# A two-layer decoder trunk: the written order of the feed-forward input stage extended to its first block and to the output stage's first loads, and one product moved to another PSUM bank

## The chip, the cores and the metric

The kernel runs on one core of one Trainium2 chip. A core has TensorE (matrix products, written PE in the profile, its weight loads PEld), VectorE (DVE), ScalarE (ACT), GpSimd (POOL), SyncE (SP) and 16 DMA engines that SP, POOL and ACT feed through queues of their own. On-chip data lies in SBUF, products land in PSUM, which has eight banks of 512 float32 per partition. The metric is the time of one execution on the device in microseconds, lower is better.

## The reference

Two decoder layers over 512 positions of width 1024. Each layer has a mixer, a cross attention into 256 memory rows and a SwiGLU feed-forward part, each between two RMS norms. All of it is float32. The change touches the feed-forward part:

```python
def swiglu(h, w_gu, w_down):
    g, u = jnp.split(h @ w_gu, 2, axis=-1)
    return (jax.nn.silu(g) * u) @ w_down

# in each layer:
h = rmsnorm(x, g_ffn_pre[layer])
y = swiglu(h, w_ffn_gu[layer], w_ffn_down[layer])
x = x + rmsnorm(y, g_ffn_post[layer])
```

`w_gu` is 1024 x 5632 (2816 gate and 2816 up columns), `w_down` 2816 x 1024.

## The kernel before

**Products.** To keep float32 accuracy each operand is split into a rounded high part (a cast on ACT, "hi") and the rest (a subtraction on DVE, "lo"), and each product is three matmuls, high by high, high by low, low by high (`mm3`, lines 299 to 301).

**The feed-forward input stage** computes g and u, transposed, in blocks of 256 columns: 11 blocks of the gate and 11 of the up half, numbered jp 0 to 10. Block 0 of both is computed by `ws_gemm_split` while the rows of the cross attention before it are still being normed and transposed. Its two results end in `act(0, ...)`: a Silu on ACT and a multiply on DVE for each of two halves, and a store of the product y to DRAM from POOL's queue.

**The stream.** The other 20 blocks ("chunks", gate and up in turn) go through `Winograd.stream`, which computes a 2 x 2 block product with 7 products in place of 8. One factor is made of sums of the transposed rows h: n1, n3, s2, n4 (`sums`, 4 subtractions, each with a split into hi and lo), once for all chunks. The other is made of sums of the chunk's weights: t3, t2, t1, t4 (`prepare`, line 432, DVE), split into four pairs hi1 to hi4 (ACT, line 441) and lo1 to lo4 (DVE, line 442). `hi1`/`lo1` hold b11 and t1, the first and third product's weights; `hi2`/`lo2` t2; `hi3`/`lo3` t3 and t4; `hi4`/`lo4` b21 and b22. While the products of one chunk run, the next chunk's weights are prepared, and the chunk after that is loaded from DRAM on SP (`wr`, two loads of 512 KB).

The seven products of a chunk, in order, are a11 b11, s2 t2, n1 t1, n3 t3, a12 b21, a22 t4, n4 b22, each 12 matmuls of 256 columns. They write halves of four banks, `bks[0]` to `bks[3]`; gate chunks use four banks named bB, up chunks four named bA. DVE combines them: q and then u and v (line 455), and the four quarters of the result (`out`: line 827 for gate, 835 for up). Quarter (0, two) reads the fifth product, quarter (0, one) the sixth, and quarter (1, both) the seventh and the third, as `tail` at the start of the next chunk. A gate chunk ends in a Silu on ACT (829), an up chunk in a multiply on DVE (837) and a store of y to DRAM (810).

**The output stage** (`OutProj`, final product with `w_down`) runs y as the stationary operand against 512 weight columns. In `half0_steps` it takes the 22 rows of blocks two at a time: `load_w` loads and splits 512 KB of weights, and `parts`, called `LEAD` = 2 steps ahead, loads back 512 KB of y and splits it. Both come over SP's queue into the pool `wst` of four staging buffers, which the stream also uses for t3 and t4 (`tt`) and for y before its store (`yr`).

**What sets the order.** TensorE's instructions stand in the order in which the code issues them. Inside `stream` that holds for ACT and DVE too (`manual_schedule`): the names that `do(...)` lists between the products are their queue order. Elsewhere a scheduler orders ACT, DVE and the queues by its own estimates, and the pools decide which buffer a tile gets and what it must wait for. Each engine takes its queue strictly in turn.

Of the kernel before, what the change touches and what calls it, by code (L numbers as in the profile page):

```python
# [15 lines left out]
P = 128  # L16
# [9 lines left out]
LEAD = 2  # L26
# [16 lines left out]
def trunk_kernel(ctx: ExitStack, tc: tile.TileContext, a: dict, out: bass.AP):  # L43
# [32 lines left out]
    def f(ap):  # L76
        return ap.bitcast(F32)
# [295 lines left out]
    class Winograd:  # L373
# [7 lines left out]
            self.hT = hT  # L381

        def sums(self):
            hT = self.hT
            r0, r1 = hT.raw
            e, l = slice(0, 256), slice(256, 512)
            a21, a11, a22, a12 = r0[:, :, e], r0[:, :, l], r1[:, :, e], r1[:, :, l]
            sub = lambda o, i0, i1: nc.vector.tensor_tensor(out=o, in0=i0, in1=i1, op=ALU.subtract)
            self.parts = {}
            sub(a22, a21, a22)  # L390
            sub(a21, a21, a11)
            sub(a11, a11, a22)
            for name, raw in (("s2", a11), ("n1", a22), ("n3", a21)):
                self.put(name, raw)
            sub(a12, a12, a11)
            self.put("n4", a12)
            for name, hf, half in (("a11", 0, 1), ("a12", 1, 1), ("a22", 1, 0)):
                q = hT.quads[hf][half]
                self.parts[name] = q[:, :, 0:256], q[:, :, 256:512]

        def put(self, name, raw):
            g = group("wa")
            self.parts[name] = g[:, :, 0:256], g[:, :, 256:512]
            split_out(raw, *self.parts[name])

        def load(self, w, c0):
            raw = f(group("wr")).rearrange("p a (b c) -> p (a b) c", c=256)
# [6 lines left out]
        def prepare(self, r):  # L414
# [22 lines left out]
                "t4": add(tt[:, :, one], t2, r1[:, :, one]),  # L437
            }

            def part(src, to):  # L440
                return (lambda: nc.scalar.copy(out=to[0], in_=src),  # L441
                        lambda: nc.vector.tensor_tensor(out=to[1], in0=src, in1=f(to[0]), op=ALU.subtract))  # L442

            for i, (src, to) in raws.items():
                steps[f"hi{i}"], steps[f"lo{i}"] = part(src, to)
# [3 lines left out]
        def stream(self, chunks):  # L449

# [4 lines left out]
            tt = lambda o, i0, i1, op: nc.vector.tensor_tensor(out=o, in0=i0, in1=i1, op=op)  # L455
            raws = [self.load(*ch[:2]) for ch in chunks[:2]]
            ws, steps = self.prepare(raws[0])
            for s in ("t3", "t2", "t1", "t4", "hi1", "hi2", "hi3", "hi4", "lo1", "lo2", "lo3", "lo4"):
                steps[s]()
            self.sums()  # L460
            tail = lambda: None
            for n, (w, c0, bank, out) in enumerate(chunks):
                if n + 2 < len(chunks):
                    raws.append(self.load(*chunks[n + 2][:2]))
                nxt, steps = self.prepare(raws[n + 1]) if n + 1 < len(chunks) else (None, {})

# [18 lines left out]
                nc.scalar.copy(out=p1, in_=ps)  # L485
# [33 lines left out]
    class OutProj:  # L519
        def __init__(self, w, y, nk, g_post, g_pre, hT, first=bankA, second=bankB, final=False):  # L520
# [3 lines left out]
            self.first, self.second = first, second  # L524
            self.banks = None
            self.tails = {}
            self.ahead = self.gate = None
            self.hs = [None] * NT

# [8 lines left out]
        def half0_steps(self, ks, first, last):  # L538

            if first:  # L540
                with tc.issue_after(self.gate) if self.gate else nullcontext():
                    self.g_post = load_gain(self.gains[0])
                self.banks = [self.first() for _ in range(NT)]
            if self.ahead:
                for k in ks[:LEAD]:
                    self.ahead(k)
# [250 lines left out]
    def ffn(layer, hT, prev, proj):  # L797
# [1 line left out]
        y = Feat([None] * NFF, [None] * NFF)  # L799

        y2 = dram.tile([P, NFF, 512], F32, name=f"y2_{layer}")
        yraw = {}

        def y_rows(jp):

# [3 lines left out]
        def put_y(jp):  # L809
            nc.gpsimd.dma_start(out=y2[:, 2 * jp:2 * jp + 2, :], in_=yraw[jp])  # L810

        def act(jp, gb, ub):
            y_ = y_rows(jp)
            for m in range(2):
                s = sbuf("sw")
                nc.scalar.activation(out=s, in_=gb[m], func=AF.Silu)
                nc.vector.tensor_tensor(out=y_[:, m, :], in0=s, in1=ub[m], op=ALU.mult)
            put_y(jp)

        def chunks(jp):  # L820
# [10 lines left out]
            def up(m, sl, ps, sb, op):  # L831
# [1 line left out]
                    y_.append(y_rows(jp))  # L833
                ym = y_[0][:, m, :]
                nc.vector.tensor_tensor(out=ym[:, sl], in0=ps, in1=sb, op=op)  # L835
                if sl.start == 0:
                    nc.vector.tensor_tensor(out=ym, in0=ym, in1=s[m], op=ALU.mult)
                    if m == 1:
                        put_y(jp)

            return [(w, jp * 256, bankB, gate), (w, FF + jp * 256, bankA, up)]

        def parts(jp):
            yg = group("y")
            src = wst.tile([P, 2, 512], F32, tag="st", name="yr")
            nc.sync.dma_start(out=src, in_=y2[:, 2 * jp:2 * jp + 2, :])
            split_out(src, yg[:, 0:2, :], yg[:, 2:4, :])
# [4 lines left out]
        act(0, gb, ub)  # L852
        with tc.manual_schedule(engines={mybir.EngineType.Activation, mybir.EngineType.DVE}):
            Winograd(hT).stream([c for jp in range(1, NFF // 2) for c in chunks(jp)])
        proj.y = y
        proj.ahead = lambda k: parts(k // 2)
        proj.run()
# [424 lines left out]
```

## Time and profile before

| | |
|---|---|
| time, median of 3 runs | 1508.97 us (1508.11 to 1509.59) |
| the profiled execution | 1508.91 us |
| its span, first to last instruction | 1507.1 us |
| mean granted clock of TensorE | 0.978 |
| DMA, mean over the span | 116 GB/s |
| feed-forward input stages: the stream of 20 chunks | from 420.9 and from 1133.9 us |
| output stages that follow | from 664.2 and from 1377.3 us |

Profile lines give, for a group of instructions or a single one, line and engine, what it writes and reads, the shape, and its time; a bracket at the end tells how long the engine stood idle before it and which instruction released it. A DVE or ACT instruction's length is longer than the step to the next one, since the next starts before the last one has drained. TensorE's matmuls overlap in the same way, so the pitch between starts counts, not the length. The granted clock is the share of TensorE's full clock.

### The profile page before, as it was taken

The numbers are of one execution on the slowest core, as the hardware profiler recorded it, in microseconds if no ns is written. First come the engines' busy times: TensorE is split into PE (matmuls) and PEld (weight loads), VectorE is DVE, ScalarE is ACT, GpSimd is POOL, SyncE is SP. The second block draws the span as 40 slices with busy tenths as digits, with TensorE's granted clock in tenths as the row PEclk, the third lists the DMA queues.
The fourth block names the chain that finished last, engine by engine and source line by source line (L and its number), as shares of the span: only waits on it lengthen the run. The fifth ranks groups of instructions, "written<-read, shape, count | busy, mean of one in ns | idle before, by whom it ended". The sixth has DMA issues, their size and how long they took to land.

```text
span 1507.1 us, 21475 instructions
## 1 busy us (share of the span) xinstructions
PE 1433.4 (95%) x8564; PEld 1267.0 (84%) x8564; DVE 1023.5 (68%) x1623; ACT 665.7 (44%) x1069; POOL 49.4 (3%) x104
## 2 busy tenths in 40 slices
PE   8999999999979999979999999999997999997998
PEld 6777789888969999968889888988896999996886
DVE  5785767455679888853447998645558888885332
ACT  4354555334544443433334886534444344434330
POOL 1000000000100000000010000000010000000000
PEclk9999999999979999989999999999997999998999
DMA  5533254421313333255512235442122342425521
GB/s 167 180 99 91 70 169 132 142 79 58 116 65 117 111 128 114 97 181 192 159 48 96 80 112 175 137 150 71 56 84 71 112 140 99 140 85 189 175 84 56
DMA packets 125726, 174.33 MB, mean 116 GB/s; under 512 B 6885, under 2 KB 88881, under 8 KB 125626
## 3 DMA queue, kind: packets, MB, share of 16 engines
q1 hardware_dynamic: 117890, 152.46, 31.8%
q0 software_dynamic: 3840, 13.65, 2.4%
q10 hardware_dynamic: 3896, 6.86, 1.4%
q8 instruction: 67, 1.10, 0.3%
q14 instruction: 33, 0.27, 0.1%
HBM read 159.29 MB, written 13.65 MB: 115 GB/s over the span
## 4 chain that ended last, share of the span: by engine, by line
PE 82%; DVE 13%; issue 3%; DMA 1%; ACT 1%; DVEq 0%; POOLq 0%; SPq 0%; ACTq 0%
PE bA L299 13%; PE bA L301 12%; PE bA L300 12%; PE bB L535 5%; PE bB L536 5%; PE bB L534 5%; PE bA L534 5%; PE bA L536 5%; PE bA L535 5%; PE bB L299 3%; PE bB L300 2%; PE bB L301 2%; DVE wl L442 2%; DVE tt L432 2%; DVE yr L835 2%
## 5 line engine op out<-in xcount | busy, mean ns | idle before, releaser
L511 DVE TENSOR_TENSOR wl<-st,wh 128x1024 fp32r<-128x1024 f32 x148 | 180.6, 1223 | 192.9 <-ACT wh L510 190.7
L510 ACT CAST wh<-st 128x1024 fp32r<-128x1024 f32 x148 | 155.5, 1051 | 240.1 <-PE bA L300 66.1
L299 PE MATMUL bA<-hTh,wh 128*128 128x512 f32 (+1 forms) x448 | 171.4, 383 | 0.0
L301 PE MATMUL bA<-hTh,wl 128*128 128x512 f32 (+1 forms) x448 | 168.0, 375 | 0.0
L300 PE MATMUL bA<-hTl,wh 128*128 128x512 f32 (+1 forms) x448 | 167.7, 374 | 0.0
L441 ACT CAST wg<-wr 128x1024 fp32r<-128x1024 f32 x80 | 83.6, 1045 | 41.4 <-DVE wr L432 41.4
L534 PE MATMUL bB<-wh,y 128*128 128x512 f32 x208 | 83.1, 399 | 17.0 <-ACT wh L510 17.0
L442 DVE TENSOR_TENSOR wg<-wr,wg 128x1024 fp32r<-128x1024 f32 x80 | 97.3, 1216 | 0.0
L301 PEld LDWEIGHTS bA<-hTh,wl 128*128 128x128 f32 x448 | 84.3, 188 | 15.3
L300 PEld LDWEIGHTS bA<-hTl,wh 128*128 128x128 f32 x448 | 84.6, 189 | 13.6
L299 PEld LDWEIGHTS bA<-hTh,wh 128*128 128x128 f32 x448 | 84.5, 189 | 13.5
L535 PE MATMUL bB<-wl,y 128*128 128x512 f32 x208 | 82.8, 398 | 0.9 <-DVE wl L511 0.9
L536 PE MATMUL bB<-wh,y 128*128 128x512 f32 x208 | 82.4, 396 | 0.0
L299 PE MATMUL bA<-hTq,wh 128*128 128x256 f32 x208 | 61.2, 294 | 10.3 <-DVE yr L835 10.3
L534 PEld LDWEIGHTS bB<-wh,y 128*128 128x128 f32 x208 | 40.1, 193 | 25.8 <-ACT wh L510 17.4
L829 ACT ACTIVATE sw<-sw 128x512 f32<-128x512 f32 x40 | 25.3, 633 | 78.3 <-DVE sw L827 78.3
L301 PE MATMUL bA<-hTq,wl 128*128 128x256 f32 x208 | 58.7, 282 | 0.0
L300 PE MATMUL bA<-hTq,wh 128*128 128x256 f32 x208 | 58.7, 282 | 0.0
L299 PE MATMUL bB<-wa,wh 128*128 128x256 f32 x160 | 46.9, 293 | 12.1 <-ACT wa L510 11.1
L534 PE MATMUL bA<-wh,y 128*128 128x512 f32 x144 | 56.5, 392 | 0.0
L536 PE MATMUL bA<-wh,y 128*128 128x512 f32 x144 | 56.1, 390 | 0.0
L535 PE MATMUL bA<-wl,y 128*128 128x512 f32 x144 | 56.1, 389 | 0.0
(329 smaller groups left out, 4212.6 us busy)
## 6 DMA issues: line engine op xcount, KB each, us to landing
wr<-in_w_ffn_gu_dram SPq DMA_DIRECT2D x80, 512.0 KB, 4.6
st<-in_w_ffn_down_dram SPq DMA_DIRECT2D x44, 512.0 KB, 4.3
st<-in_w_xkv_dram SPq DMA_DIRECT2D x32, 512.0 KB, 4.4
st<-in_ab_w_in_dram SPq DMA_DIRECT2D x24, 512.0 KB, 3.8
y<-yr POOLq DMA_DIRECT2D x22, 512.0 KB, 3.9
yr<-y SPq DMA_DIRECT2D x22, 512.0 KB, 4.7
st<-in_w_xq_dram SPq DMA_DIRECT2D x16, 512.0 KB, 3.4
st<-in_w_xo_dram SPq DMA_DIRECT2D x16, 512.0 KB, 3.8
```

What stands on the lines that cost most here:

```text
L299: nc.tensor.matmul(out=ps, lhsT=wh, rhs=xh, start=first, stop=False)
L300: nc.tensor.matmul(out=ps, lhsT=wh, rhs=xl, start=False, stop=False)
L301: nc.tensor.matmul(out=ps, lhsT=wl, rhs=xh, start=False, stop=last)
L432: add = lambda o, i0, i1: lambda: nc.vector.tensor_tensor(out=o, in0=i0, in1=i1, op=ALU.add)
L441: return (lambda: nc.scalar.copy(out=to[0], in_=src), lambda: nc.vector.tensor_tensor(out=to[1], in0=src, in1=f(to[0]), op=ALU.subtract))
L442: lambda: nc.vector.tensor_tensor(out=to[1], in0=src, in1=f(to[0]), op=ALU.subtract))
L510: nc.scalar.copy(out=hi, in_=src)
L511: nc.vector.tensor_tensor(out=lo, in0=src, in1=f(hi), op=ALU.subtract)
L534: nc.tensor.matmul(out=ps, lhsT=yh, rhs=wh[:, kk, :], start=first, stop=False)
L535: nc.tensor.matmul(out=ps, lhsT=yh, rhs=wl[:, kk, :], start=False, stop=False)
L536: nc.tensor.matmul(out=ps, lhsT=yl, rhs=wh[:, kk, :], start=False, stop=last)
L835: nc.vector.tensor_tensor(out=ym[:, sl], in0=ps, in1=sb, op=op)
```

## The change

The diff has five parts, which act in both layers.

1. `sums` no longer issues its instructions but returns them as named steps, and `stream` writes them, the first chunk's preparation and the two Silus of block 0 in one list. The two multiplies and the store of block 0 (`act`) become the first chunk's `tail`. POOL's queue is now ordered by hand too inside the stream.
2. In the loop t1 with hi1 trades places with t2 with hi2, t4 with hi3 moves behind lo4, and in up chunks the multiply of the first half moves behind lo3.
3. The fifth product goes to the second half of `bks[1]` in place of the second half of `bks[3]`.
4. y comes back in blocks of four rows (1 MB) into groups of the pool `gpool`, from POOL's queue, in place of 512 KB from SP's into `wst`. The first such load is issued three chunks before the end, two more in the last chunk.
5. In the last chunk the first two weight blocks of the output stage are loaded, and they and the first two blocks of y are split there, as steps a to d.

```diff
         def sums(self):
...
+            steps = {"n1": sub(a22, a21, a22), "n3": sub(a21, a21, a11),
+                     "s2": sub(a11, a11, a22), "n4": sub(a12, a12, a11)}
...
+                steps["hi_" + name], steps["lo_" + name] = self.split_steps(raw, to)
...
-            for s in ("t3", "t2", "t1", "t4", "hi1", "hi2", "hi3", "hi4", "lo1", "lo2", "lo3", "lo4"):
+            steps.update(self.sums(), **extra)
+            for s in ("n1", "n3", "s2", "hi_n1", "hi_s2", "t3", "t1", "t2", "hi1", "t4", "lo_n1", "hi2", "act0", "lo_s2",
+                      "lo1", "hi4", "lo2", "act1", "hi_n3", "hi3", "n4", "lo_n3", "lo3", "hi_n4", "lo4", "lo_n4"):
                 steps[s]()
-            self.sums()
-            tail = lambda: None
+            tail = then
...
+                steps.update(side(len(chunks) - 1 - n))
...
-                do("t2", "hi2")
+                do("t1", "hi1")
                 ps = product(bks[1][:, one], "s2", "t2")
                 tt(q, ps, p1, ALU.subtract)
-                do("t1", "hi1", "t4", "hi3")
+                do("t2", "hi2", "a")
                 ps = product(bks[2][:, one], "n1", "t1")
                 tt(u, ps, q, ALU.add)
-                do("lo4")
+                do("lo4", "t4", "hi3", "b")
                 ps = product(bks[0][:, two], "n3", "t3")
                 tt(v, ps, q, ALU.add)
-                do("lo2")
-                ps = product(bks[3][:, two], "a12", "b21")
+                do("lo2", "c")
+                ps = product(bks[1][:, two], "a12", "b21")
                 out(0, two, ps, p1, ALU.add)
-                do("lo1")
+                do("lo1", "d")
                 ps = product(bks[3][:, one], "a22", "t4")
-                out(0, one, ps, v, ALU.subtract)
+                end = out(0, one, ps, v, ALU.subtract)
                 do("lo3")
+                if end:
+                    end()
...
+                wt = self.ready.pop(k) if k in self.ready else load_w(self.w, k, 2, 0, 512)
                 if self.ahead:
...
-                wt = load_w(self.w, k, 2, 0, 512)
...
+        def load_y(i):
+            n = min(4, NFF - 4 * i)
+            yback[i] = f(group("yb"))
+            nc.gpsimd.dma_start(out=yback[i][:, 0:n, :], in_=y2[:, 4 * i:4 * i + n, :])
...
+        def side(left):
+
+            if left == 3:
+                load_y(0)
+            if left:
+                return {}
+            raw = [load_raw(proj.w, k, 2, 0, 512) for k in (0, 2)]
+            for i in (1, 2):
+                load_y(i)
...
+            return {"a": lambda: weights(0), "b": lambda: parts(0), "c": lambda: weights(1), "d": lambda: parts(1)}
```

**VectorE at the start of the stream, layer 0.** Before, from the last rows of the stage ahead (hTq is the low part of the transposed rows); L817 is the multiply of block 0, L432 a sum of weights, L442 a low part of weights, L388 a sum of rows (n1, n3, s2, then n4) and L511 its low part:

```order
L293 TENSOR_TENSOR hTq<-bB,hTq 128x4x128 x2
L817 TENSOR_TENSOR yr<-sw,bA 128x512
L432 TENSOR_TENSOR tt<-wr 128x4x128
L432 TENSOR_TENSOR t_3856<-tt,wr 128x512
L432 TENSOR_TENSOR wr<-wr 128x4x128
L432 TENSOR_TENSOR tt<-t_3856,wr 128x4x128
L817 TENSOR_TENSOR yr<-sw,bA 128x512
L442 TENSOR_TENSOR wg<-wr,wg 128x1024
L442 TENSOR_TENSOR wl<-t_3856,wh 128x512
L442 TENSOR_TENSOR wl<-tt,wh 128x1024
L442 TENSOR_TENSOR wg<-wr,wg 128x1024
L388 TENSOR_TENSOR raw<-raw 128x4x256 x3
```

Now, from n3 on (n1 stands further up, between two hTq steps); L387 is a sum of rows, L430 a sum of weights, L402 every low part, L812 the multiply of block 0:

```order
L387 TENSOR_TENSOR raw<-raw 128x4x256
L293 TENSOR_TENSOR hTq<-bB,hTq 128x4x128 x2
L387 TENSOR_TENSOR raw<-raw 128x4x256
L430 TENSOR_TENSOR tt<-wr 128x4x128
L430 TENSOR_TENSOR wr<-wr 128x4x128
L430 TENSOR_TENSOR t_3850<-tt,wr 128x512
L430 TENSOR_TENSOR tt<-t_3850,wr 128x4x128
L402 TENSOR_TENSOR wa<-raw,wa 128x4x256 x2
L402 TENSOR_TENSOR wg<-wr,wg 128x1024
L402 TENSOR_TENSOR wl<-t_3850,wh 128x512
L387 TENSOR_TENSOR raw<-raw 128x4x256
L812 TENSOR_TENSOR yr<-sw,bA 128x512 x2
```

Between the last two of these rows stand the four remaining low parts. The multiplies of block 0 moved from the front to the end, and the sums of rows from the end to the front.

**TensorE between the fifth and the sixth product of the first chunk, layer 0.** The number in a name tells banks apart. Before, last three matmuls of the fifth product and first three of the sixth:

```order
L299 MATMUL bB_3906<-hTq_2640,wg_3863 128x256
L300 MATMUL bB_3906<-hTq_2640,wg_3863 128x256
L301 MATMUL bB_3906<-hTq_2640,wg_3863 128x256
L299 MATMUL bB_3906<-hTq_2639,wh_3861 128x256
L300 MATMUL bB_3906<-hTq_2639,wh_3861 128x256
L301 MATMUL bB_3906<-hTq_2639,wl_3862 128x256
```

Now:

```order
L299 MATMUL bB_3900<-hTq_2640,wg_3857 128x256
L300 MATMUL bB_3900<-hTq_2640,wg_3857 128x256
L301 MATMUL bB_3900<-hTq_2640,wg_3857 128x256
L299 MATMUL bB_3902<-hTq_2639,wh_3855 128x256
L300 MATMUL bB_3902<-hTq_2639,wh_3855 128x256
L301 MATMUL bB_3902<-hTq_2639,wl_3856 128x256
```

The two products no longer share a bank; 3900 is also the bank of the second product, whose result is q.

**The queues at the end of the stream, layer 0.** SP before, from the last chunk's weights (wr) on; yr is y coming back, st weights of the output stage:

```order
L411 DMA wr_5998<-in_w_ffn_gu_dram 128x4x256
L846 DMA yr_6356<-y2_0_3577 128x1024
L846 DMA yr_6361<-y2_0_3577 128x1024
L846 DMA yr_6366<-y2_0_3577 128x1024
L119 DMA st_6370<-in_w_ffn_down_dram 128x2x512
L846 DMA yr_6401<-y2_0_3577 128x1024
L119 DMA st_6405<-in_w_ffn_down_dram 128x2x512
```

SP now:

```order
L409 DMA wr_6000<-in_w_ffn_gu_dram 128x4x256
L119 DMA st_6245<-in_w_ffn_down_dram 128x2x512
L119 DMA st_6247<-in_w_ffn_down_dram 128x2x512
L119 DMA st_6433<-in_w_ffn_down_dram 128x2x512
L119 DMA st_6466<-in_w_ffn_down_dram 128x2x512
```

POOL now, where before only the stores stood (y2 is y in DRAM, yb y coming back, the row from yr_6336 the last store):

```order
L807 DMA y2_0_3577<-yr_5595 128x1024
L842 DMA yb_5884<-y2_0_3577 128x2048
L807 DMA y2_0_3577<-yr_5843 128x1024
L807 DMA y2_0_3577<-yr_6093 128x1024
L842 DMA yb_6249<-y2_0_3577 128x2048
L842 DMA yb_6251<-y2_0_3577 128x2048
L842 DMA yb_6505<-y2_0_3577 128x2048
L807 DMA y2_0_3577<-yr_6336 128x1024
L842 DMA yb_6573<-y2_0_3577 128x2048
L842 DMA yb_6641<-y2_0_3577 128x1024
```

The weights of the output stage stand right behind the stream's last weights on SP, and the returns of y moved to POOL, among the stores.

More of the change, by code (lines that the diff above doesn't have):

```diff
@@ L438, in prepare, with stream @@
             }
-            def part(src, to):
-                return (lambda: nc.scalar.copy(out=to[0], in_=src),
-                        lambda: nc.vector.tensor_tensor(out=to[1], in0=src, in1=f(to[0]), op=ALU.subtract))
             for i, (src, to) in raws.items():
-                steps[f"hi{i}"], steps[f"lo{i}"] = part(src, to)
+                steps[f"hi{i}"], steps[f"lo{i}"] = self.split_steps(src, to)
             return {"b11": (w1, one), "t1": (w1, two), "t2": (w2, one), "t4": (w3, one),
                     "t3": (w3, two), "b21": (w4, one), "b22": (w4, two)}, steps
-        def stream(self, chunks):
+        def stream(self, chunks, extra, then, side):
             one, two = slice(0, 256), slice(256, 512)
@@ L835, in up @@
                 nc.vector.tensor_tensor(out=ym[:, sl], in0=ps, in1=sb, op=op)
[L836 to L839, printed above, removed]
+                mult = lambda: nc.vector.tensor_tensor(out=ym, in0=ym, in1=s[m], op=ALU.mult)
+                if m == 1:
+                    mult()
+                    put_y(jp)
+                return mult if sl.start == 0 else None
@@ L841, in chunks @@
             return [(w, jp * 256, bankB, gate), (w, FF + jp * 256, bankA, up)]
+        def load_y(i):
+            n = min(4, NFF - 4 * i)
+            yback[i] = f(group("yb"))
+            nc.gpsimd.dma_start(out=yback[i][:, 0:n, :], in_=y2[:, 4 * i:4 * i + n, :])
         def parts(jp):
+            if jp // 2 not in yback:
+                load_y(jp // 2)
             yg = group("y")
[L845 to L846 removed]
@@ L847, in parts, with weights @@
-            split_out(src, yg[:, 0:2, :], yg[:, 2:4, :])
+            split_out(yback[jp // 2][:, jp % 2 * 2:jp % 2 * 2 + 2, :], yg[:, 0:2, :], yg[:, 2:4, :])
             for m in range(2):
                 y.hi[2 * jp + m], y.lo[2 * jp + m] = yg[:, m, :], yg[:, 2 + m, :]
-        gb, ub = ws_gemm_split(w, [0, FF], hT, prev.hook)
-        act(0, gb, ub)
-        with tc.manual_schedule(engines={mybir.EngineType.Activation, mybir.EngineType.DVE}):
-            Winograd(hT).stream([c for jp in range(1, NFF // 2) for c in chunks(jp)])
+        def side(left):
[6 more added lines that the diff above has]
+                load_y(i)
+            def weights(n):
+                proj.ready[2 * n] = split_w(raw[n], 2, 512)
+            return {"a": lambda: weights(0), "b": lambda: parts(0), "c": lambda: weights(1), "d": lambda: parts(1)}
@@ new lines, in ffn @@
+        gb, ub = ws_gemm_split(w, [0, FF], hT, prev.hook)
+        with tc.manual_schedule(engines={mybir.EngineType.Activation, mybir.EngineType.DVE, mybir.EngineType.Pool}):
+            first = [sbuf("sw") for _ in range(2)]
+            silu = lambda m: lambda: nc.scalar.activation(out=first[m], in_=gb[m], func=AF.Silu)
+            Winograd(hT).stream([c for jp in range(1, NFF // 2) for c in chunks(jp)],
+                                {"act0": silu(0), "act1": silu(1)}, lambda: act(0, first, ub), side)
```

37 lines of the change are left out of this document (14 added, 23 removed).

## The prediction

> **What bounds the kernel now.** I read the page's busy line and chain first, then TensorE's waits, then the time line around them.
>
> ```profile
> PE 1433.4 (95%) x8564; PEld 1267.0 (84%) x8564; DVE 1023.5 (68%) x1623; ACT 665.7 (44%) x1069; POOL 49.4 (3%) x104
> PE 82%; DVE 13%; issue 3%; DMA 1%; ACT 1%; DVEq 0%; POOLq 0%; SPq 0%; ACTq 0%
> ```
>
> TensorE (PE) carries 82% of the chain; the 13% of VectorE (DVE) are the places where TensorE waits for it. The view of TensorE's waits, cut to the feed-forward stage of layer 0 (415 to 680 us), shows them; columns are engine and line, who released it, total us, times, longest.
>
> ```profile
> PE bB L299 <- DVE sw L827: 8.5, 10, 2.5
> PE bB L534 <- ACT wh L510: 8.5, 1, 8.5
> PE bB L299 <- ACT wa L510: 5.4, 1, 5.4
> PE bA L299 <- DVE yr L835: 5.2, 10, 0.5
> PE bB L299 <- ACT wg L441: 1.0, 1, 1.0
> PE bB L301 <- DVE wg L442: 0.8, 1, 0.8
> PE bB L300 <- DVE wa L511: 0.7, 1, 0.7
> PE bB L299 <- ACT wx L485: 0.5, 1, 0.5
> PE bB L535 <- DVE wl L511: 0.5, 1, 0.5
> ```
>
> Three places: ten waits each on L827 and L835 inside the stream of products (13.7 us), the first chunk's operands (1.0 + 0.8 + 5.4 + 0.7 + 0.5 = 8.4), and the first weights of the output stage (8.5 + 0.5 = 9.0). Together 31.1 us; layer 1 repeats them. The waits also cost clock, as stretches of the time line show (us, busy us of PE, PEld, DVE, ACT, POOL, granted clock, DMA share, GB/s):
>
> ```profile
> 421.00:424.00 3.00, 1.26 (x7) 0.97 (x7) 3.00 (x5) 3.00 (x4) 0.59 (x1) 0.94 0.14 57
> 431.00:437.40 6.40, 5.72 (x24) 5.25 (x24) 5.24 (x5) 3.54 (x4) 0.00 (x0) 0.51 0.01 3
> 444.00:447.60 3.60, 3.60 (x20) 3.60 (x19) 2.10 (x3) 0.92 (x2) 0.00 (x0) 0.53 0.00 0
> 664.20:669.20 5.00, 4.49 (x10) 3.21 (x11) 4.45 (x4) 3.14 (x3) 0.00 (x0) 0.50 0.85 291
> 480.81:502.67 21.86, 20.67 (x171) 20.27 (x170) 19.28 (x31) 9.14 (x12) 0.53 (x1) 1.00 0.36 121
> ```
>
> Half clock after each long gap; full clock in a settled pair of chunks (last row), where VectorE works 19.28 of 21.86 us. That row matters most below: VectorE is nearly full as well.
>
> **What a stage without waits takes.** TensorE's time line gives the pitch.
>
> ```profile
> 480.80 0.28 PE L299 MATMUL bB<-hTq,wg 128*128 128x256 f32 x1
> 487.88 0.28 PE L301 MATMUL bB<-hTq,wg 128*128 128x256 f32 x1
> 420.81 0.28 PE L301 MATMUL bA<-hTq,wl 128*128 128x256 f32 x1
> 669.48 0.40 PE L535 MATMUL bB<-wl,y 128*128 128x512 f32 x1
> 679.94 0.39 PE L536 MATMUL bB<-wh,y 128*128 128x512 f32 x1
> 1133.79 0.28 PE L301 MATMUL bA<-hTq,wl 128*128 128x256 f32 x1
> 1382.90 0.40 PE L536 MATMUL bB<-wh,y 128*128 128x512 f32 x1
> ```
>
> The first two rows are the first and the 60th matmul of a chunk: 7.08 / 59 = 0.120 us. A chunk (7 products of 12) is 10.08, a pair 20.16. At 420.81 the stage before the stream issues its last matmul, at 669.48 the output stage its 11th, after which it runs freely, 46 steps to 679.94, 0.2274 each. With no wait, 20 chunks put the output's first matmul at 420.81 + 1681 x 0.120 = 622.53 and its 11th at 624.80: 44.7 us earlier. In layer 1 (1133.79; 1382.90 is the 12th) it is 1335.51 + 2.50 = 1338.01 against 1382.90: 44.9. So 89.6 us are at stake, 62 of them waits, the rest half clock and slow restarts.
>
> **The change part by part.**
>
> *The bank.* The sixth product (a22, t4) waits for L827 or L835, which reads the other half of its bank. Moved to bank 1, the fifth product must instead wait for the read of q there, which comes two products earlier. So both kinds of wait go. What is late next is VectorE's last operand for the next chunk, lo1 (L442, wg):
>
> ```profile
> 481.76 0.68 DVE L835 TENSOR_TENSOR yr<-bA,wy 128x512 f32<-128x512 f32 x1
> 488.36 0.42 DVE L827 TENSOR_TENSOR sw<-bB,wx 128x256 f32<-128x256 f32 x1
> 488.69 1.22 DVE L442 TENSOR_TENSOR wg<-wr,wg 128x1024 fp32r<-128x1024 f32 x1
> ```
>
> Here VectorE began the chunk's first step 0.96 after TensorE (481.76 - 480.80) and ended lo1 at 489.91, 8.15 later. The new order puts the same operations ahead of lo1 (t1 and t2, and lo4 and t4, trade places), so the 8.15 stands. With TensorE unbroken, the sixth product ends 8.8 into a chunk; its subtraction (0.33), lo3 (1.14) and the multiply moved behind lo3 (0.60) end at 10.9, 0.8 into the next chunk; lo1 ends at 9.0, and is wanted with the third matmul of the following chunk, at 10.32. Slack 1.3 us: 0 lost. The cover is VectorE's 20.16 - 19.28 = 0.88 us a pair; if gone, every us too much is a us of TensorE.
>
> *The first chunk.* Same operations, earlier and sorted by need. Pitches and the place where VectorE comes free:
>
> ```profile
> 407.41 0.69 DVE L293 TENSOR_TENSOR hTq<-bB,hTq 128x512 fp32r<-128x512 f32 x1 [1.64 <-ACT hTq L292]
> 408.39 0.69 DVE L293 TENSOR_TENSOR hTq<-bB,hTq 128x512 fp32r<-128x512 f32 x1 [0.29 <-ACT hTq L292]
> 418.32 0.69 DVE L817 TENSOR_TENSOR yr<-sw,bA 128x512 f32<-128x512 f32 x1 [9.24 <-PE bA L301]
> 420.25 0.68 DVE L432 TENSOR_TENSOR wr<-wr 128x512 f32<-128x512 f32 x1
> 420.86 0.68 DVE L432 TENSOR_TENSOR tt<-t,wr 128x512 f32<-128x512 f32 x1
> 423.79 1.22 DVE L442 TENSOR_TENSOR wl<-tt,wh 128x1024 fp32r<-128x1024 f32 x1
> 424.93 1.22 DVE L442 TENSOR_TENSOR wg<-wr,wg 128x1024 fp32r<-128x1024 f32 x1
> ```
>
> VectorE idled 9.24 us behind L817, which stood first in its queue. Steps of 512 follow at 0.60, of 1024 at 1.14, of 256 at 0.33 (488.36 to 488.69). Now n3 slips ahead of the two hTq steps, mostly into the 1.64 us idle, and VectorE is free at about 409.3. Then s2, four adds, lo_n1, lo_s2, lo1: 4 x 1.14 + 4 x 0.60 + 0.24 for two dependent steps = 7.2, so 416.5; TensorE wants lo1 at 421.2. lo2 and five steps of 1024 end at 422.8; the fourth product wants lo3, the third of these five, at 425.5, the seventh lo_n4, the last, at 429.6. ACT beside it:
>
> ```profile
> 408.38 1.28 ACT L816 ACT_TABLE_LOAD   x1
> 420.97 1.04 ACT L441 CAST wg<-wr 128x1024 fp32r<-128x1024 f32 x1 [5.00 <-DVE wr L432]
> ```
>
> ACT idled 5.00 us until VectorE had t1; now its casts (1.04 at most), the table load (1.28) and two Silus run between 409 and 420 in the order of VectorE's steps. The cast for t2 needs a weight buffer that the stage before holds until the 36th of its last 96 matmuls (about 413.7); from there hi2, the table load, both Silus, hi4 and hi_n3 add up to 4.9 (512 wide taken as half of 1.04), less what overlaps, so lo_n3, due at 418.2, waits some 0.3 for its cast and the row ends at 423.1. All in time, so 8.4 us of waits go, and with them the half clock. The two multiplies of L817 come last (to 424.3). They take VectorE's lead: eleven steps of the next chunk (five of 512, four of 256, lo4 and lo1, one dependent: 6.8 us) end lo1 at 431.1, wanted at 431.25. That is the thinnest place: a slip of 1 us in twenty steps would cost TensorE 0.9, none costs 0; I take 0.1, by the walk. n1 stands ahead of one hTq step of the stage before and delays what follows there by at most its own 1.14, while TensorE has a block of 24 matmuls (2.9 us) to run: 0 to 1.1, I take 0.1, nearer to the cover.
>
> *The output's first loads.* Before, three returns of y took three of the four staging buffers, and the first weights could only be asked for when VectorE had split one:
>
> ```profile
> 658.38 0.38 SPq L119 DMA_DIRECT2D st<-in_w_ffn_down_dram  x1
> 663.14 1.04 ACT L510 CAST wh<-st 128x1024 fp32r<-128x1024 f32 x1 [13.54 <-DMA st<-in_w_ffn_down_dram]
> st<-in_w_ffn_down_dram SPq DMA_DIRECT2D x44, 512.0 KB, 4.3
> y<-yr POOLq DMA_DIRECT2D x22, 512.0 KB, 3.9
> ```
>
> Now y returns through POOL into groups of its own (six loads for eleven, 1 MB each but one), and the weights stand in SP's queue right behind those of the last chunk, whose buffers VectorE frees two chunks before the end. 4.3 us fit well within 10; two weight blocks and two y blocks are split in the last chunk, where VectorE and ACT have no next chunk to prepare (5.3 us of steps gone, four pairs added). TensorE starts with 48 matmuls, 10.9 us. The second y load waits for a group of the chunk before last, so leaves by about 612.5; no row has a 1 MB load, so between one and two times 3.9 us, nearer 7.8 by size: there by 620.3, wanted at 633.4. POOL's later stores wait behind these loads, but the last is read back 30 us later. Cost 0; without that cover, up to the 9.0 us plus 2.2 of half clock again.
>
> **Sum.** 1508.91 (the profiled run; span 1507.1, median of runs 1508.97) - 44.7 - 44.9 + 2 x 0.2 = 1419.7; I say 1420.
>
> [...]
>
> **Rivals.** (1) *VectorE becomes the bound.* For it: 19.28 of 20.16, and its queue waits in order for q, u, v. Against: the 1.3 us slack. If half of the 1.70 a pair stays (21.86 - 20.16), 9 pairs x 0.85 x 2 = 15: 1435. (2) *The output stage still starts late*, because y loads and weights meet on the DMA engines (share 0.85 at 664) or a group is freed late: half of 11.2 a layer is 1431, all 1442. Against: 10 us of lead. (3) *The bank is not what those waits are for.* Then 27.4 us stay, and restarts: about 1450. Against: the releaser is exactly that read. (4) *Slower:* lo1 falls so far behind in VectorE's queue that every chunk waits. It decides at 89 / 39 = 2.3 us a chunk, lo1 3.6 later than walked; at 4.5 later, 39 x 3.2 = 125, 1545. Against: the set ahead of lo1 is unchanged.
>
> **How the numbers follow.** Forecast 0.76 (own range 1416 to 1424: measurement, 0.3%), rival 1 0.11, rival 2 0.07, rival 3 0.03, rival 4 0.02, no change 0.01. The range 1416 to 1436 takes in the forecast and rival 1, leaving about 0.1 out. Faster by over 0.2% (what a measurement of this kernel can tell) 0.97, within 0.01, slower 0.02.
>
> **What would show it.** Right: no wait on the two DVE reads in TensorE's waits, a pair of chunks of 20.2 us, granted clock 1.00 from 421 to the output stage, the first L534 matmul at about 622.6, wh's cast ahead of it by microseconds. Wrong: pairs above 20.5 with waits for wg (rival 1), a wait for wh, wl or y at the output's start (2), waits for the DVE reads (3).

## The result, and the profile after

| | before | after |
|---|---|---|
| time, median of the runs shown with the result (us) | 1508.54 (1506.35 to 1509.59, 4 runs) | 1418.61 (1418.34 to 1419.26, 4 runs) |
| ratio, with its 95% interval | | 0.9406 (0.939 to 0.9423) |
| the profiled execution, its span (us) | 1508.91, 1507.1 | 1419.26, 1417.5 |
| mean granted clock | 0.978 | 0.997 |

The forecast was 1420. The busy line and the chain of the page after:

```profile
PE 1406.5 (99%) x8564; PEld 1252.3 (88%) x8564; DVE 1013.9 (72%) x1623; ACT 663.6 (47%) x1069; POOL 55.9 (4%) x116
...
PE 99%; DMA 1%; ACT 0%; DVE 0%; DVEq 0%; POOLq 0%; issue 0%; SPq 0%; ACTq 0%
```

VectorE's 13% of the chain are gone. The view of TensorE's waits, now over the whole run, has three rows left (engine and line, releaser, total us, times, longest):

```profile
PE bB L283 <- DVE h L236: 1.6, 2, 1.2
PE bA L905 <- ACT hTh L292: 1.5, 1, 1.5
PE bB L892 <- POOL ident masks.py:199: 1.5, 1, 1.5
```

None lies in the stream or at the output stage's start. The stretches (us, busy us of PE, PEld, DVE, ACT, POOL, granted clock, DMA share, GB/s) show the first chunk and a settled pair at full clock:

```profile
420.00:431.00 11.00, 11.00 (x94) 11.00 (x93) 10.96 (x16) 4.41 (x6) 0.59 (x1) 1.00 0.41 144
441.20:461.36 20.16, 20.16 (x170) 20.16 (x170) 19.00 (x31) 9.12 (x12) 0.54 (x1) 1.00 0.40 131
```

The pair of 21.86 us has become one of 20.16. VectorE has no idle time to speak of in the first row and 1.16 us in the second. The time line after has the two moments on which the prediction's sum and its thinnest place rest (start us, length, engine, line, operation):

```profile
429.95 1.22 DVE L402 TENSOR_TENSOR wg<-wr,wg 128x1024 fp32r<-128x1024 f32 x1
...
431.00 0.28 PE L300 MATMUL bA<-hTq,wg 128*128 128x256 f32 x1
431.22 0.38 PE L301 MATMUL bA<-hTq,wg 128*128 128x256 f32 x1
431.45 0.28 PE L299 MATMUL bA<-hTq,wg 128*128 128x256 f32 x1
...
622.59 0.40 PE L534 MATMUL bB<-wh,y 128*128 128x512 f32 x1
```

lo1 of the second chunk ended at 431.17. The matmul that reads it started 0.22 us after its neighbour, and the next 0.23 later, in place of 0.12 each: 0.2 us lost, and that is all that the stream of layer 0 loses. The output stage's first matmul came at 622.59.

### The profile page after: what moved, and what is told of

Read it like the earlier page. It is cut to its first block, busy times and chain, and to the rows that moved or that the text cites. A ratio compares the mean times of both kernels' runs of the same rounds, so it can differ in the third digit from the quotient of the medians.

```text
span 1417.5 us, 21486 instructions
## 1 busy us (share of the span) xinstructions
PE 1406.5 (99%) x8564; PEld 1252.3 (88%) x8564; DVE 1013.9 (72%) x1623; ACT 663.6 (47%) x1069; POOL 55.9 (4%) x116
## 4 chain that ended last, share of the span: by engine, by line
PE 99%; DMA 1%; ACT 0%; DVE 0%; DVEq 0%; POOLq 0%; issue 0%; SPq 0%; ACTq 0%
PE bA L299 14%; PE bA L301 14%; PE bA L300 14%; PE bB L300 6%; PE bB L299 6%; PE bB L301 6%; PE bA L534 5%; PE bA L536 5%; PE bA L535 5%; PE bB L535 5%; PE bB L534 5%; PE bB L536 5%; PE bA L905 2%; PE bB L283 1%; PE bA L697 1%; PE bA L699 1%
## 5 line engine op out<-in xcount | busy, mean ns | idle before, releaser
L402 DVE TENSOR_TENSOR wg<-wr,wg 128x1024 fp32r<-128x1024 f32 x80 | 97.4, 1217 | 0.0
L534 PE MATMUL bB<-wh,y 128*128 128x512 f32 x208 | 80.9, 389 | 0.0
L536 PE MATMUL bB<-wh,y 128*128 128x512 f32 x208 | 80.9, 389 | 0.0
L401 ACT CAST wh<-tt 128x1024 fp32r<-128x1024 f32 x40 | 42.1, 1052 | 61.2 <-DVE tt L430 61.2
L402 DVE TENSOR_TENSOR wl<-tt,wh 128x1024 fp32r<-128x1024 f32 x40 | 48.7, 1219 | 0.0
```

The lines of the kernel that those rows point to most:

```text
L401: return (lambda: nc.scalar.copy(out=to[0], in_=src), lambda: nc.vector.tensor_tensor(out=to[1], in0=src, in1=f(to[0]), op=ALU.subtract))
L534: nc.tensor.matmul(out=ps, lhsT=yh, rhs=wh[:, kk, :], start=first, stop=False)
L536: nc.tensor.matmul(out=ps, lhsT=yl, rhs=wh[:, kk, :], start=False, stop=last)
```

## The experiments

First the three edits one by one. Settled pairs are measured from the first matmul of a chunk to that of the next but one.

**The bank alone, on the kernel before.**

```diff
-                ps = product(bks[3][:, two], "a12", "b21")
+                ps = product(bks[1][:, two], "a12", "b21")
```

> The kernel before with one edit: the fifth product of each chunk goes to the second half of bank 1 in place of bank 3. My account: the 20 waits a layer on the two DVE reads go (13.7 us of the waits, and the restarts: 1.70 us for each of nine settled pairs, 2.5 for the first chunk), nothing else; the first chunk and the output's first loads stay as they are. About 17 us a layer, so 1508.5 - 34 = 1474 us (1470 to 1478); a settled pair 20.2 us; TensorE's waits keep wh 8.5 and wa 5.4. Rival 1 (VectorE is the bound): pairs stay above 20.5 with waits for wg, 1490 or more. Rival 3 (the bank isn't what those waits are for): 1508.5, pairs of 21.86.

Measured: 1469.62 us (1468.51 to 1469.94), 38.0 under the runs of before beside it (1507.65), 4 us more gain than expected. TensorE's waits from 415 to 680 us, and a settled pair:

```profile
PE bB L534 <- ACT wh L510: 8.5, 1, 8.5
PE bB L299 <- ACT wa L510: 6.2, 1, 6.2
...
```

```profile
474.22:494.38 20.16, 20.16 (x171) 20.16 (x169) 19.09 (x31) 9.03 (x12) 0.53 (x1) 1.00 0.39 131
```

The waits on the DVE reads are gone and nothing took their place. The other two kinds stay: 8.5 for wh as before, 6.2 for wa where it was 5.4. Rivals 1 and 3 fall. Most of the 4 us lie in the first pair of chunks, which takes 32.7 us where it took 36.9 (4.2 less, 2.5 expected). Of that stretch TensorE was busy 11.0 us at half clock before (granted clock 0.50 from 423.66 to 437.31 and from 444.14 to 447.56) and is busy 4.6 us at half clock here (0.50 from 425.38 to 435.62).

**The bank undone, on the changed kernel** (the same line, back).

> The changed kernel with only the fifth product back in bank 3. My account: twenty waits a layer on the subtraction of the fifth product return, some 1.7 us a pair and 2 us in the first chunk, with half clock after that one: 17 to 19 us a layer, 1418.6 + 36 = 1455 us (1451 to 1459), pairs of about 21.8. Rival 3: 1418.6, pairs of 20.16.

Measured: 1458.58 us (1458.22 to 1459.94), 40.0 over the changed kernel; the range expected ended at 1459. Its waits, and a pair:

```profile
PE bB L299 <- DVE sw L822: 15.5, 20, 1.9
PE bA L299 <- DVE yr L830: 12.9, 20, 0.7
```

```profile
454.39:476.35 21.96, 20.67 (x171) 20.27 (x169) 19.27 (x31) 9.23 (x13) 0.53 (x1) 1.00 0.36 121
```

Forty waits of 28.4 us cost 40.0. The pair shows the rest: of 21.96 us TensorE idles 21.96 - 20.67 = 1.29, while 20.67 stands for work that takes 20.16 unbroken. That is 0.51 a pair, 0.25 for each wait, a cost beyond the idle time that is listed. Forty times 0.25 and the 28.4 make 38.4; of the other 1.6, a stretch of half clock in layer 1 (granted clock 0.50 from 1117.75 to 1121.17) makes 1.5, estimated from pitches: in the kernel before, matmuls of 256 columns stand 0.213 us apart at granted clock 0.50 (444.49 to 445.77, seven starts) in place of 0.120, so the 16 of such a stretch lose 0.093 each.

**The output part undone.** y returns as before, and the last chunk loads and splits nothing for the output stage.

```diff
-            if left == 3:
-                load_y(0)
-            if left:
-                return {}
+            return {}
...
-            split_out(yback[jp // 2][:, jp % 2 * 2:jp % 2 * 2 + 2, :], yg[:, 0:2, :], yg[:, 2:4, :])
+            src = wst.tile([P, 2, 512], F32, tag="st", name="yr")
+            nc.sync.dma_start(out=src, in_=y2[:, 2 * jp:2 * jp + 2, :])
+            split_out(src, yg[:, 0:2, :], yg[:, 2:4, :])
...
+            if self.ahead:
+                for k in ks[:LEAD]:
+                    self.ahead(k)
```

> The changed kernel with y returned as before (512 KB each from SP's queue into the staging buffers, two steps ahead) and no output weights or y loaded or split in the last chunk. My account: the wait of 8.5 to 9 us for the output's first weights returns in each layer with 2.2 us of half clock: 1418.6 + 22.4 = 1441 us (1438 to 1444). If the stream's faster end leaves VectorE no earlier for the first weights, up to 1446. Rival: the early loads do little because y would have come in time anyway; below 1430.

Measured: 1443.15 us (1442.95 to 1444.38), 24.5 over the changed kernel. Waits from 590 to 650 us, and the output stage's first stretch:

```profile
PE bB L534 <- ACT wh L509: 8.8, 1, 8.8
PE bB L535 <- DVE wl L510: 0.5, 1, 0.5
```

```profile
630.50:637.47 6.97, 6.51 (x14) 4.75 (x15) 4.88 (x4) 3.91 (x4) 0.00 (x0) 0.50 0.84 280
```

The wait is back at its old size. Half clock lasted 7.0 us into the stage here, over 14 matmuls; of 512 columns they start 0.427 us apart (632.35 to 634.91) in place of the 0.2274 of the prediction, so 2.8 us is lost. In the kernel before, it lasted over 10 matmuls and took 2.0 us (the prediction has 2.2, half of the busy time in its row from 664.2 to 669.2). In layer 1 half clock ended 4.7 us into the stage, where it ended 5.5 us into it before (at 1382.81), and took no more. So it makes 0.8 of the 2.1 us between 22.4 and 24.5; the rest was not taken apart; the four waits would add 0.25 us each if they cost as much beyond the idle time listed as those with the bank undone.

**Only the output's weights late.** y still returns early; the first two weight blocks are left to the output stage.

```diff
-            raw = [load_raw(proj.w, k, 2, 0, 512) for k in (0, 2)]
...
-            return {"a": lambda: weights(0), "b": lambda: parts(0), "c": lambda: weights(1), "d": lambda: parts(1)}
+            return {"b": lambda: parts(0), "d": lambda: parts(1)}
```

> The changed kernel in which y still returns early by POOL into its own groups and is split in the last chunk, but the output's first two weight blocks are loaded and split by the output stage as before. My account: what held the first weights were the staging buffers that returned y took; with y elsewhere their load is early, so only the subtraction for wl stands behind the stream's last reads: 0 to 2.5 us of wait a layer, 1419 to 1425. Rival (the split in the last chunk is what pays): near the 1443 of the kernel with the whole part undone.

Measured: 1431.51 us (1431.26 to 1433.21), between my account and the rival. Where the wait is (TensorE's waits, then VectorE's time line):

```profile
PE bB L535 <- DVE wl L510: 8.3, 2, 4.1
```

```profile
620.49 1.21 DVE L510 TENSOR_TENSOR y<-yb,y 128x1024 fp32r<-128x1024 f32 x1
...
621.96 1.21 DVE L510 TENSOR_TENSOR y<-yb,y 128x1024 fp32r<-128x1024 f32 x1
...
624.29 1.21 DVE L510 TENSOR_TENSOR y<-yb,y 128x1024 fp32r<-128x1024 f32 x1
625.42 0.68 DVE L831 TENSOR_TENSOR yr<-yr,sw 128x512 f32<-128x512 f32 x1
626.02 3.48 DVE L510 TENSOR_TENSOR wl<-st,wh 128x1024 fp32r<-128x1024 f32 x3
```

The wait for the first load (wh) is gone, so with y in groups of its own the staging buffers are free in time: SP issues the weights' first load at 603.1. That is worth 1443.15 - 1431.51 = 11.6 us (the first two blocks of y are also split in the last chunk here, which this run doesn't part from it). But the first wl now stands behind splits of y that are not wanted for long, and TensorE waits 4.1 us for it in each layer, with half clock for 3.4 us behind it (granted clock 0.50 from 627.36 to 630.77). So splitting the weights in the last chunk is worth 1431.51 - 1418.61 = 12.9 us. My account had only the stream's last reads ahead of wl.

**The first block undone.** Silus and multiplies of block 0 stand ahead of the stream, then the first chunk's weights, then the sums.

```diff
-            steps.update(self.sums(), **extra)
-            for s in ("n1", "n3", "s2", "hi_n1", "hi_s2", "t3", "t1", "t2", "hi1", "t4", "lo_n1", "hi2", "act0", "lo_s2",
-                      "lo1", "hi4", "lo2", "act1", "hi_n3", "hi3", "n4", "lo_n3", "lo3", "hi_n4", "lo4", "lo_n4"):
+            for s in ("t3", "t2", "t1", "t4", "hi1", "hi2", "hi3", "hi4", "lo1", "lo2", "lo3", "lo4"):
                 steps[s]()
-            tail = then
+            sums = self.sums()
+            for s in ("n1", "n3", "s2", "hi_s2", "lo_s2", "hi_n1", "lo_n1", "hi_n3", "lo_n3", "n4", "hi_n4", "lo_n4"):
+                sums[s]()
+            tail = lambda: None
...
+        act(0, first, ub)
```

> The changed kernel with the first block as before: the Silus and multiplies of block 0 ahead of the stream, then the first chunk's weights, then the sums of the rows, in the order of before on VectorE. My account: the first chunk waits for b11, t2, n3 and on again (8.4 us were the waits put down to operands before, some 13 with those that hang on them), and half clock after each: 16 us a layer, 1418.6 + 32 = 1451 us (1445 to 1454), the settled pairs still 20.16. Rival (the waits cost only themselves, no clock): 1418.6 + 2 x 8.4 = 1435.

Measured: 1445.27 us (1444.78 to 1445.38), 26.7 over the changed kernel, nearly 6 less than expected and at the lower end of the range. Waits from 408 to 680 us:

```profile
PE bB L299 <- ACT wa L401: 6.2, 1, 6.2
PE bB L299 <- ACT wx L483: 1.3, 1, 1.3
PE bB L299 <- ACT wg L401: 1.0, 1, 1.0
PE bB L301 <- DVE wg L402: 0.8, 1, 0.8
PE bB L300 <- DVE wa L402: 0.7, 1, 0.7
PE bA L301 <- DVE wg L402: 0.3, 1, 0.3
```

10.3 us a layer of the 13.3 that it costs. In layer 0 the granted clock is 0.50 from 427.75 to 434.58, with 16 matmuls in it: 1.5 us at the pitches above. Six restarts at 0.25, as an estimate from the kernel with the bank undone, make another 1.5. The three parts together: 40.0 + 24.5 + 26.7 = 91.2, against 89.9 for the whole (1508.54 - 1418.61). They add up to within 1.3 us; they touch different stretches of the run.

**Only the old order of the list**, Silus and multiplies behind it as the change has them:

```diff
+            for s in ("t3", "t2", "t1", "t4", "hi1", "hi2", "hi3", "hi4", "lo1", "lo2", "lo3", "lo4",
+                      "act0", "act1", "n1", "n3", "s2", "hi_s2", "lo_s2", "hi_n1", "lo_n1", "hi_n3", "lo_n3", "n4", "hi_n4", "lo_n4"):
```

> The changed kernel with Silus and multiplies of block 0 where the change put them (behind the first chunk's preparation), but the first chunk's weights all ahead of the sums of the rows, as before the change. My account, by walking VectorE's queue from 409 us: it is free at once, lo3 waits for its cast until 416.3, s2 is summed at 422.0 and split at 424.3 where TensorE wants it at 422.2 (2 us of wait), the row and the two multiplies end at 431 and lo1 of the second chunk at 438, wanted at 433.3 (4.7 us of wait), with half clock after it: 7 to 10 us a layer, 1433 to 1439. If the sorting by need is worth nothing: 1418.6.

**Only Silus and multiplies ahead**, the sorted list kept (`act(0, first, ub)` outside the stream, `tail = lambda: None`):

> The changed kernel with the new sorted list, but Silus and multiplies of block 0 ahead of the stream as before. My account: VectorE stands behind the first multiply until the last matmul of block 0 (418.3 us) again, lo1 of the first chunk ends at 425.4 where it is wanted at 421 (4.3 us of wait), lo1 of the second at 438.7, wanted at 435.8 (2.9 us), with half clock: 9 to 11 us a layer, 1437 to 1441. If the sums ahead of it save most of that: below 1430.

Measured: 1432.67 us (1432.4 to 1432.82) and 1432.96 us (1432.56 to 1434.17). The waits of the two, 408 to 680 us:

```profile
PE bB L299 <- ACT wx L482: 2.7, 1, 2.7
PE bB L299 <- ACT wa L401: 1.0, 1, 1.0
PE bB L300 <- DVE wa L402: 0.9, 1, 0.9
```

```profile
PE bB L301 <- DVE wg L402: 3.8, 1, 3.8
PE bB L299 <- DVE wx L449: 0.7, 1, 0.7
PE bB L299 <- ACT wg L401: 0.4, 1, 0.4
PE bA L301 <- DVE wg L402: 0.2, 1, 0.2
```

Each half of the part is worth about 14 us (14.1 and 14.3), together 28.4 against 26.7 for both. Both runs came out under their ranges, the first by 0.3 us, the second by 4. In the first, s2's 1.9 us came as walked, but the second wait was of another kind: the fourth product waited for ScalarE's copy of the first product (wx), whose bank it shares and which stood behind late casts in ScalarE's queue. In the second, the first chunk waited 3.8 for lo1 (4.3 walked), and the second chunk hardly (0.2, where 2.9 was walked).

**The loop's order undone**, bank and all else kept:

```diff
-                do("t1", "hi1")
+                do("t2", "hi2")
...
-                do("t2", "hi2", "a")
+                do("t1", "hi1", "t4", "hi3", "a")
...
-                do("lo4", "t4", "hi3", "b")
+                do("lo4", "b")
...
-                do("lo3")
                 if end:
                     end()
+                do("lo3")
```

> The changed kernel with the loop's old written order (t2 with hi2 ahead of t1 with hi1, t4 and hi3 ahead of lo4, the up chunk's multiply ahead of lo3), all else kept. My account: the same operations stand ahead of lo1, so the order within the loop is worth nothing: 1418.6 us (1417.5 to 1420), pairs of 20.16, no wait for wg. Rival: the order is what lets the bank pay (lo1 or the reads come late without it); then 1424 or more, with waits for wg, wh or wl in the pairs.

Measured: 1418.57 us (1417.86 to 1419.06), the same as the changed kernel, and no wait in the stream. The trades of places in the loop are worth nothing measurable.

**VectorE's cover**, by repeating an addition whose result does not change, two, three and four times in every chunk:

```diff
-                do("t2", "hi2", "a")
+                do("t2", "t2", "hi2", "a")
```

> The changed kernel with the addition for t2 (512 wide, 0.60 us) written twice in every chunk: 1.20 us more of VectorE a pair, against 1.16 us that it has left (19.00 busy of 20.16). My account: TensorE still sets the pace, 1420 us (1418.6 to 1424), with one wait of about 0.5 us at the second chunk, where the slack was under 0.1. Rival (VectorE is already the bound, because its queue stands still for q, u and v): each pair longer by about 1.2, 2 x 9.5 x 1.2 = 23 us, 1441.

> The changed kernel with the addition for t2 written three times in every chunk: 2.4 us more of VectorE a pair, 1.42 beyond the cover of 0.98 that the kernel with it twice showed (pairs of 20.38 for 1.20 us more). In the kernel with it four times half clock followed only slots of 3.41 us in which TensorE was idle for 1.9 us or more, and none with 1.8 or less. By that reading one wait of 1.2 to 1.5 us a pair brings no half clock: clock 1.00 in the stream, pairs of 21.6 to 21.9, 1418.6 + 2 x (0.9 + 9 x 1.4 to 1.7) = 1446 to 1452 us. Rival (any wait of more than 1 us brings half clock, as the prediction used it): pairs of up to 23.3, 1460 or more; on the straight line between twice (1423.7) and four times (1492.6) it would be 1458.

> The changed kernel with that addition written four times in every chunk: 3.6 us more of VectorE a pair, 2.4 beyond its cover. My account: each us too much is a us of TensorE, 9.5 pairs x 2.4 = 23 us a layer, 1418.6 + 46 = 1465 us, and up to 0.29 us a wait on top (what each of the 40 waits of the kernel with the bank undone cost beyond its length), 1476; pairs of 22.6 to 23.1. Rival (idle time between VectorE's steps can take it up): below 1450.

Measured: 1423.71 us (1423.54 to 1423.93), 1451.63 (1451.21 to 1452.19) and 1492.55 (1489.36 to 1494.9). Pairs of the first two, one kernel after the other:

```profile
441.08:461.46 20.38, 20.38 (x171) 20.21 (x169) 20.21 (x33) 9.24 (x12) 0.54 (x1) 1.00 0.39 130
```

```profile
441.92:463.74 21.82, 20.58 (x171) 20.26 (x169) 21.58 (x35) 9.24 (x12) 0.54 (x1) 1.00 0.35 121
```

From chunk start to chunk start pairs take 20.38, 21.82 and 23.0 to 24.8 us. With 1.20 us of added work a pair, 0.22 shows, so the cover is 0.98. (The first row has TensorE busy throughout: a matmul is drawn 0.28 us long at a pitch of 0.12, so a stop of up to 0.16 does not show as idle time.) With 2.40, 1.42 is too much and 1.66 shows. With 3.60, 2.62 is too much, and some pairs take 23.04, 2.88 longer. So each us too much costs a us, and about 0.25 on top. The pairs of 24 and more do not fit that: they have half clock (seven stretches of 3.41 us between 420 and 660 us at granted clock 0.50), and the kernel as a whole took 16 us more than the upper end of what was expected (1476). Two equal waits of that kernel, and the stretches in which they lie, each as long as the windows of half clock seen there:

```profile
502.48 0.28 PE L300 MATMUL bA<-hTq,wg 128*128 128x256 f32 x1
504.73 0.39 PE L301 MATMUL bA<-hTq,wg 128*128 128x256 f32 x1 [1.97 <-DVE wg L402]
504.95 0.28 PE L299 MATMUL bA<-hTq,wg 128*128 128x256 f32 x1
...
553.67 0.39 PE L301 MATMUL bA<-hTq,wg 128*128 128x256 f32 x1 [1.97 <-DVE wg L402]
```

```profile
502.31:505.72 3.41, 1.44 (x12) 1.24 (x12) 3.41 (x6) 1.67 (x3) 0.00 (x0) 1.00 0.00 0
505.72:509.14 3.42, 3.42 (x18) 3.42 (x18) 2.34 (x5) 2.88 (x5) 0.00 (x0) 0.50 0.93 305
...
550.09:553.50 3.41, 1.61 (x14) 1.41 (x12) 3.41 (x6) 1.05 (x1) 0.00 (x0) 1.00 0.02 5
553.50:556.92 3.42, 3.25 (x27) 3.25 (x28) 3.38 (x6) 2.47 (x4) 0.00 (x0) 1.00 0.57 178
```

Both waits are 1.97 us. The first lies within one stretch of 3.41 us, which leaves TensorE 1.44 busy, and the next stretch runs at 0.50. The second reaches over the stretch's end by 0.17, leaves 1.61 busy, and the clock stays 1.00. The kernel with the addition three times was run on that reading: its waits of up to 1.4 us brought no half clock, and 1451.63 lies in the range that it gave (1446 to 1452), not at the 1460 of the rival, which took half clock to follow any wait of more than 1 us, as it followed waits of 1.0 and 0.8 us in the kernel before (granted clock 0.50 from 423.66).

**One late place only**: the addition seven times in the first chunk, once elsewhere.

```diff
+                do(*["t2"] * (1 if n else 7), "hi2", "a")
```

> The changed kernel with that addition written seven times in the first chunk alone (3.6 us more ahead of lo1 of the second chunk, whose slack was under 0.1). My account: waits of 1.1 us (last product of the first chunk) and 2.4 us (second chunk, wg) a layer, 3.5 + 2 x 0.3 = 4.1, so 1426.8 us by the waits alone; if half clock follows a 3.4 us stretch in which TensorE was mostly idle, 1.7 us more a layer at times: up to 1430. If the slack of the second chunk is larger than walked: below 1424.

Measured: 1428.7 us (1427.08 to 1429.84), 10.1 over. The two waits of layer 0 on the time line, and the second of layer 1:

```profile
431.49 0.39 PE L299 MATMUL bB<-wa,wg 128*128 128x256 f32 x1 [1.85 <-DVE wy L449]
...
435.63 0.58 PE L301 MATMUL bA<-hTq,wg 128*128 128x256 f32 x1 [1.88 <-DVE wg L402]
...
1110.43 0.39 PE L301 MATMUL bA<-hTq,wg 128*128 128x256 f32 x1 [2.20 <-DVE wg L402]
```

The waits expected were 1.1 and 2.4 us. In layer 0 both were followed by half clock, from 432.9 to 439.7. In layer 1 the same two places waited 1.85 and 2.20 us, and the clock stayed 1.00: the longer wait, from 1108.23 to 1110.43, lies across an edge at 1108.75 (198 stretches of 3.413 us after 432.91; edges at 423.66 and 1160.94 in the kernel before lie 737.28 apart, 216 such stretches), so that no stretch has more than 1.7 us idle. After the first chunks the pairs were 20.16: a loss there is paid once.

## Why the prediction was right, step by step

- **The sum.** The way of adding up, the pitch of a free stage in place of the list of waits, held to a few tenths: first output matmul at 622.59 for 622.53, a pair of 20.16, 1418.61 for 1420. It needed no size for any one part.
- **The bank.** Right in mechanism (nothing took the wait's place) and in "the same operations stand ahead of lo1": the loop's order undone changes nothing. Its share was never priced in the sum, only in rival 3 as 27.4 us of waits "and restarts", about 1450; the run with the bank undone gives 1458.6. The waits measured there were 28.4, and the restarts made most of the rest.
- **VectorE's cover.** 0.88 a pair was forecast, 0.98 measured. "Every us too much is a us of TensorE" holds up to waits of 1.4 us. Behind waits of 1.97 half clock came on top in some places, so by these runs rival 4's price was too low.
- **The first chunk.** The thinnest place was the right one: lo1 ended at 431.17 (forecast 431.1), and 0.2 us was lost where 0.1 was taken. Doubling the addition once (0.60 us) made it a wait of 0.7, so there was no slack left. The delay through n1 cannot be told apart: TensorE waits for h 0.4 to 2.6 us in all in the kernels run, 1.6 in the changed one and 2.6 in the one with the first block undone, where n1 stands late again. Removing the idle time behind the first multiply and sorting the list count alike, which the prediction did not say.
- **The output's first loads.** "Up to 9.0 plus 2.2 a layer" was 12.3 (24.5 / 2): waits of 9.3, and half clock that cost 2.8 us in layer 0; the rest was not taken apart. Two steps were wrong without effect. The VectorE steps that the last chunk no longer has are not 5.3 us but 6.4 by the prediction's own pitches (five of 0.60, three of 1.14). The other is on POOL's time line, with the second load of y, the last store and the load that reads it back:

```profile
605.82 0.54 POOL L842 DMA_DIRECT2D yb<-y  x1 [0.17 <-issue]
...
626.32 0.54 POOL L807 DMA_DIRECT2D y<-yr  x1 [7.05 <-DVE yr L831]
...
630.27 0.54 POOL L842 DMA_DIRECT2D yb<-y  x1 [2.85 <-DMA y<-yr]
```

The second load left at 605.8, ahead of 612.5, and a load of 1 MB took 7.0 us (the median of the profile's 12), close to the 7.8 taken. But the last store was read back 4 us later, not 30. That cost nothing, because TensorE wants that block only with the last of its eleven steps, 10 x 24 matmuls of 0.2274 us (the prediction's pitch), 55 us after 622.59.
- **The clock.** The granted clock was 1.00 up to the output stage, as forecast (1.00 in the row from 420.00 and over 431.30 to 623.00). In the runs with waits under 3.4 us the length alone does not decide what follows (1.85 us brought half clock and 2.20 did not, in one kernel): it went with how much of a stretch of 3.41 us the wait fills. The edges of the stretches keep a fixed step: in the kernel with four additions, half clock begins and ends 14 times between 420 and 660 us, each time a multiple of 3.413 us after the first edge, at 434.04; the last is at 628.60, 194.56 or 57 stretches on. Three of these edges, in slices of 0.5 us (PE busy, granted clock):

```profile
485.00:485.50 0.50, 0.50 (x6) 0.76 0.02 4
...
505.50:506.00 0.50, 0.50 (x5) 0.72 0.25 35
...
509.00:509.50 0.50, 0.50 (x6) 0.86 0.22 68
```

A mean of 0.76 that rises from half to full puts the edge at 485.24, the 0.72 that falls at 505.72, the 0.86 at 509.14: 20.48 and 3.42 apart, six stretches and one. The stretch before 505.72 was idle for 1.97 of its 3.41 us, and half clock followed.

## What to carry to other kernels

Price a chain of small waits by the pitch of the undisturbed stage, not by the list of waits: here 28.4 us of listed waits cost 40.0. Before a product is written to a bank that another engine has just begun to read, look for a bank whose last read came two products earlier; the move was one line and worth 38 to 40 us, and the order around it nothing. When TensorE becomes the only bound, measure the next engine's cover by repeating a harmless instruction: it was 0.98 us in a pair of 20.16.

## What the runs showed of the hardware that was not expected

- A wait of TensorE costs some 0.25 us beyond the idle time listed for it (0.51 a pair for two with the bank undone). The time line with four additions shows of what: the matmul at 502.48 is drawn 0.28 long where the pitch is 0.12, so 0.16 us of the stop counts as busy, and the matmul behind the one that waited starts 0.22 after it, 0.10 later than at the pitch.
- Half clock came in whole windows of 3.41 us, in the kernel with four additions after windows like the first shown (1.44 us busy) and not after those like the second (1.61). In the kernel before the change it began at 423.66, after a window with only 1.7 us idle by the trace (420.25 to 423.66, TensorE busy 1.67), while that second window has 1.8. So idle time by the trace is not the whole rule, and where the limit lies stays open.
- The same wait of 1.97 us was followed by 3.41 us of half clock in one place, 1.5 us more by the pitches (16 matmuls at 0.213 for 0.120, an estimate), and by none in the other: it went by where the wait fell. The spread of the times fits that: those of the kernel before, with half clock in many places, lie between 1504.7 and 1509.6, the changed kernel's within 0.9 us. That this is the cause of the spread was not tested.
